# Down and query products with the weights stationary and the tokens moving, in one transformer block on one core

## The chip, the core and the metric

The kernel runs on one NeuronCore of a Trainium2 chip, as one launch. The metric is the device time of one execution in microseconds (us), measured outside the profiler. Beside it there is one profiled execution, whose trace is read here: the span runs from the first to the last instruction of the program. Everything is float32 in and out. Large products are made in float32r, a reduced form of float32, with each operand split in two exact halves (a high part and what is left of it), so that one float32 product is three float32r products: high by high, high by low, low by high.

## The reference, cut to what matters

One transformer block over 256 tokens of width 2048: a mixer (attention with three branches beside a gated linear recurrence) and then a feed-forward layer that picks 128 of 16,384 experts for each token. Only the feed-forward layer is touched. Its core:

```python
def peer_ffn(h, wq, keys, down, up):
    hf = h.reshape(T, D)                                            # T = 256, D = 2048
    q = (hf @ wq).reshape(T, PEER_HEADS, 2, PEER_DQ // 2)           # 8 heads, 2 halves, 128
    s = jnp.einsum('thpd,hpkd->thpk', q, keys)                      # 128 keys a half
    v1, i1 = lax.top_k(s[:, :, 0], 16); v2, i2 = lax.top_k(s[:, :, 1], 16)
    cand = v1[..., :, None] + v2[..., None, :]                      # 256 candidates a head
    vals, pick = lax.top_k(cand, 16)                                # -> expert rows eidx, softmax g
    act = gelu(einsum('td,thkd->thk', x, down[eidx])) * g
    out = einsum('thk,thkd->td', act, up[eidx])
```

The kernel does not gather rows of `down` and `up`. It multiplies all tokens by all 16,384 rows of `down`, takes the gelu, multiplies by a matrix of gate weights (expert by token, zero where an expert was not picked) and multiplies the result by all of `up`.

## The kernel before

**The stream of weights.** All weight matrices come from HBM in tiles of 128 x 2048 floats (`raw`, four buffers) that SyncE's queue loads. `next_part` splits each half of such a tile (a part: 128 x 1024, two chunks of 128 rows of the contraction by 512 columns) into `wh` (ScalarE copies with rounding, L197) and `wl` (VectorE subtracts, L198), three buffers each. `get` hands one part to the matmuls; `fill(AHEAD)` keeps two more ready.

**The products.** `block` makes one block of 512 columns for all 256 tokens: eight parts, and for each part `mm_sub` goes over two chunks and two halves of the tokens and calls `mm3`, three matmuls. The first operand of `T.matmul` after the output is the stationary one. In `mm3` it is a slice of the tokens (`xH` or `xL`, 128 contraction rows by 128 tokens) and the 512 columns of weights move, so a result lies as [128 tokens, 512 columns] in a PSUM bank, one bank for each half of the tokens. The products of the query (`wq`, four blocks) and of `down` (`d`, 32 blocks of 512 experts) are made this way; `up` (`u`) too, with `ah` and `al`, the activations, as stationary tiles.

**Behind the products.** The search for the best keys needs scores [token, key], whose contraction runs over a head's 128 query columns, and `up` needs the activations as [expert, token]. So both results are turned: `ev_wq` copies the two banks to SBUF (L1076), turns each in four transposes on TensorE (`transpose4`, L600), copies them back (L1083) and then makes the scores (L1087). `ev_d` takes the gelu of both banks (L1199), turns them in two groups of four transposes (L1207), and copies each group to `xT` (L1210). For the first 14 blocks (`LAG`), `xT` is stored in HBM (`xd`) until the gate weights are there, and loaded again later; for the others it stays in SBUF. `act` multiplies `xT` by the gate weights (L1232) and splits it into `ah` and `al`.

**The order of the work.** The program is written out in one order; the work behind the products is cut into steps (the `yield`s of a generator), put in a list of jobs by priority (`add`), and `tick`, called after every part, emits the next steps at a rate that depends on the kind of job (`RATES`). Priority 0 is `ev_wq`, `ev_d`, `ev_u`; 1 is the search on VectorE and `act`; 2 is `picks`; 3 is `w_build`, the gate weights (one-hot tables on VectorE and ScalarE, 256 float32 matmuls at L1184). The main loop makes four query blocks, 14 `down` blocks, and then in turn one `down` block and two half blocks of `up`, until `down` is done.

Of the kernel before, what the change touches and what calls it, by code (L numbers as in the profile page):

```python
# [7 lines left out]
F32 = mybir.dt.float32  # L8
# [57 lines left out]
def kernel(  # L66
# [110 lines left out]
    def load(most=RAWB):  # L177
        """Loads the stream ahead, as far as the rings allow."""
# [21 lines left out]
    def ada_load():  # L200
        """Loads ahead, as far as the rings allow."""
# [14 lines left out]
    def ada(m):  # L216
        """One chunk of a modulation vector: rows of the turned weights times the conditioning."""
        t = avs.pop(0)[1]
        V.scalar_tensor_tensor(out=t, in0=t, scalar=1.0, in1=cb, op0=OP.mult, op1=OP.mult, accum_out=m)  # L219
        n = pos["adl"]  # L220
        while (pos["adl"] < 2 * NDC or n - len(avs) > 2 * NDC) and ada_load():
            pass

    def ada_close(seg, k, n):
        """The biases; where it scales, one plus it, times the norm's gain."""
# [8 lines left out]
    def bg(r):  # L234
        """A share r of a chunk of the modulation vectors that VectorE makes beside the rest."""
# [14 lines left out]
    def adp_item():  # L250
        """A chunk of the rows of one modulation vector, in four column groups of the array."""
# [21 lines left out]
    def next_part():  # L273
        """Emits the next part of the stream; False at its end."""
# [56 lines left out]
    # steps per part of the stream, by the kind of work; the gate build's first steps go as fast as they may  # L331
# [8 lines left out]
    def finish(prio):  # L340
        """Runs the jobs up to that priority to their end."""
        while jobs and jobs[0][0] <= prio:
            step()
# [6 lines left out]
    def mm_sub(pst, kcs, wh, wl, first, last, aH, aL):  # L350
        for kk, kc in enumerate(kcs):
            for tb in range(NT):
                mm3(pst[tb], aH[:, kc, tbs[tb]], aL[:, kc, tbs[tb]], wh[:, kk], wl[:, kk],
                    first and kk == 0, last and kk == len(kcs) - 1)

# [13 lines left out]
    def rsqrt(pool, ss, n, w, name, parts=P, bufs=2):  # L369
        """1/sqrt(ss/n + eps) of a few columns, by Newton's method from an integer first guess."""  # L370
# [89 lines left out]
    def ada_first(n):  # L460
        """Chunks of the first two modulation vectors; the tokens' next two chunks when they are complete."""
# [12 lines left out]
    # two sets of four blocks, in turn over pieces of the width; the sums of the set that rests wait in SBUF  # L474
# [37 lines left out]
    def rest(b, name):  # L512
        """The rest of one of the first four blocks, added up in SBUF."""
# [18 lines left out]
    def mix(*gens, rate=0.0):  # L532
        """Steps of several pieces of work in turn."""
# [30 lines left out]
    # the compressed branch borrows what the later branches fill  # L564
# [4 lines left out]
    def table(i):  # L569
        """The rotation's tables with a norm's gains folded in."""  # L570
# [9 lines left out]
    def rope(dst, src, nh, cos, sin, name):  # L580
        """dst = src*cos + swap(src)*sin over nh heads of 128."""
# [129 lines left out]
    lw = rn.tile([P, 2, RB, P], F32, name="lw")  # L711
    G.dma_start(lw, lru_w)
    def recurrence(gr):
        n = RG
        if True:
# [19 lines left out]
            # d = 1/(1 + tanh) refined from (1 + exp)/2; decay 2d - 1; input sqrt(tanh) d (1 + ti) u  # L735
# [19 lines left out]
    held = {}  # L755

    def scores(sp, g, tb):
        """Unnormed weights of the causal and the windowed branch, and their sums."""
# [29 lines left out]
    def outputs(sp, g, tb):  # L788
        """The compressed branch's weights; all gated weights turned and times the values."""
# [281 lines left out]
    def ev_wq(j, pst):  # L1071
        """Scores of two heads; leaves them to the search."""
        res = []
        for tb in range(NT):
            qs = kq.tile([P, 512], F32, tag="qs", bufs=3, name=f"qs{j}{tb}")
            A.copy(qs, pst[tb])  # L1076
            res.append(qs)
        yield
        for tb in range(NT):
            tp = transpose4(res[tb], f"wq{j}{tb}")  # L1080
            yield
            qt = kq.tile([P, 512], F32, tag="qs", bufs=3, name=f"qt{j}{tb}")
            A.copy(qt, tp)  # L1083
            yield
            sx = ps_t(f"s{j}{tb}")
            for k in range(4):
                T.matmul(sx[:, k * P:(k + 1) * P], qt[:, k * P:(k + 1) * P], kt[:, 4 * j + k], start=True, stop=True)  # L1087
# [5 lines left out]
    def search(j, tb, sc):  # L1093
# [3 lines left out]
        # both lists are sorted: rank (a, b) has (a + 1)(b + 1) - 1 before it, so only those under 16 can be picked  # L1097
# [15 lines left out]
    def picks(tb):  # L1113
        """From places in the candidate lists to expert rows, and the softmax; heads and picks on partitions."""
# [5 lines left out]
        # place p of rank (a, b): a = max(p / 8 - 1, p / 4 - 6, 0), b = p - min(16 a, 8 a + 8, 4 a + 24)  # L1120
# [40 lines left out]
    def w_build():  # L1161
        """Gate weights by expert and token: per token the product of two one-hot tables."""
# [30 lines left out]
    xTt, wts, actH, actL = {}, {}, {}, {}  # L1193

    def ev_d(eb, pst):
        r = []
        for tb in range(NT):
            t = bp.tile([P, 512], F32, tag="ge", bufs=4, name=f"ge{eb}{tb}")
            A.activation(t, pst[tb], AF.Gelu)  # L1199
            r.append(t)  # L1200
        yield
        t = bp.tile([P, 4, S], F32, tag="xT", bufs=3, name=f"xT{eb}")
        for cc in range(2):
            tp = ps_t(f"xt{eb}{cc}")
# [207 lines left out]
```

## Time and profile before

| | |
|---|---|
| device time, median of 3 runs | 2092.45 us (2089.61 to 2093.78) |
| span of the profiled execution | 2090.6 us |
| what lies around the span, taken as median less span | 1.85 us |
| TensorE matmuls busy | 2025.0 us, 97% of the span |
| VectorE busy | 1449.4 us, 69% |
| ScalarE busy | 1053.0 us, 50% |
| moved to and from HBM | 507 MB, mean 243 GB/s |

The page of the profile gives the profiled execution by its span alone. Busy time of TensorE's matmuls is the time in which at least one matmul is in flight; a matmul's record is longer than the distance to the next one's start, so the cost of one in a row of them is read from start to start, not from its duration. PEld is the loading of stationary tiles, which has records of its own. L346 is line 346 of the kernel; a line of a helper such as `mm3` stands for all its callers, and the tile's name tells them apart.

### The profile page before, as it was taken

The page shows a single profiled execution, that of the slowest core. Times are in us where ns is not written, and L with a number is a line of the kernel's source. Part 1 is how long each engine was busy: PE and PEld are TensorE (multiplying, and loading weights), DVE is VectorE, ACT ScalarE, POOL GpSimd, SP SyncE. Part 2 cuts the span into 40 slices and gives each one's busy share as a digit, 9 for nine tenths or more (in the row PEclk, how much of TensorE's full clock was granted, in tenths as well). Part 3 has the DMA queues.
Part 4 walks back from the last instruction along what each step waited for, and adds up shares of the span by engine and source line. Part 5 has one row for each costly group of instructions (what it writes and reads, how often), then busy time and mean ns, then how long its engine had stood idle before and what let it go on. Part 6 is the DMA issues. An engine that isn't in the chain of part 4 may idle for free.

```text
span 2090.6 us, 24862 instructions
## 1 busy us (share of the span) xinstructions
PE 2025.0 (97%) x9434; PEld 1635.6 (78%) x9434; DVE 1449.4 (69%) x2149; ACT 1053.0 (50%) x1526; POOL 60.9 (3%) x95
## 2 busy tenths in 40 slices
PE   5999997999999999999999999999999999999998
PEld 4777664877888888887888888888888888888887
DVE  7888999887998666646667766665555555555566
ACT  3544676545456777854444444444444444444443
POOL 0000000000000000001000000000000000000000
PEclk8999998999999999999999999999999999999999
DMA  9897788994556666579777877765555565555563
GB/s 374 333 358 310 264 341 312 347 347 165 174 177 201 226 218 241 203 258 332 253 243 258 294 251 253 247 244 191 191 193 200 200 202 194 200 201 191 194 209 141
DMA packets 75849, 508.73 MB, mean 243 GB/s; under 512 B 8528, under 2 KB 9040, under 8 KB 20176
## 3 DMA queue, kind: packets, MB, share of 16 engines
q1 hardware_dynamic: 63792, 450.50, 60.5%
q0 software_dynamic: 11936, 56.63, 7.6%
q8 instruction: 74, 1.21, 0.2%
q14 instruction: 47, 0.39, 0.1%
HBM read 478.78 MB, written 28.31 MB: 243 GB/s over the span
## 4 chain that ended last, share of the span: by engine, by line
PE 86%; DVE 6%; issue 3%; DMA 3%; ACT 1%; POOL 0%; SPq 0%; DVEq 0%; POOLq 0%; ACTq 0%
PE d L348 11%; PE d L346 11%; PE d L347 11%; PE u L347 10%; PE u L348 10%; PE u L346 10%; PE w L1184 3%; DVE av L219 2%; DVE wl L198 2%; PE wq L346 1%; PE wq L347 1%; PE wq L348 1%; PE a L347 1%; PE a L348 1%; PE a L346 1%
## 5 line engine op out<-in xcount | busy, mean ns | idle before, releaser
L198 DVE TENSOR_TENSOR wl<-raw,wh 128x1024 fp32r<-128x1024 f32 x649 | 789.6, 1222 | 511.8 <-ACT wh L197 511.6
L197 ACT CAST wh<-raw 128x1024 fp32r<-128x1024 f32 x649 | 680.0, 1050 | 777.8 <-PE u L348 334.5
L346 PE MATMUL d<-wh,xH 128*128 128x512 f32 x1024 | 411.2, 402 | 0.0
L347 PE MATMUL d<-wl,xH 128*128 128x512 f32 x1024 | 405.1, 396 | 0.9 <-DVE wl L198 0.9
L348 PE MATMUL d<-wh,xL 128*128 128x512 f32 x1024 | 404.9, 395 | 0.0
L346 PE MATMUL u<-wh,ah 128*128 128x512 f32 x1024 | 402.1, 393 | 0.0
L347 PE MATMUL u<-wl,ah 128*128 128x512 f32 x1024 | 399.4, 390 | 1.3 <-DVE wl L198 1.2
L348 PE MATMUL u<-wh,al 128*128 128x512 f32 x1024 | 399.1, 390 | 0.0
L348 PEld LDWEIGHTS d<-wh,xL 128*128 128x128 f32 x1024 | 192.4, 188 | 45.8
L347 PEld LDWEIGHTS d<-wl,xH 128*128 128x128 f32 x1024 | 192.7, 188 | 43.9 <-DVE wl L198 1.3
L346 PEld LDWEIGHTS d<-wh,xH 128*128 128x128 f32 x1024 | 192.8, 188 | 42.6
L347 PEld LDWEIGHTS u<-wl,ah 128*128 128x128 f32 x1024 | 192.4, 188 | 41.8 <-DVE wl L198 3.0
L348 PEld LDWEIGHTS u<-wh,al 128*128 128x128 f32 x1024 | 192.2, 188 | 40.5
L346 PEld LDWEIGHTS u<-wh,ah 128*128 128x128 f32 x1024 | 192.3, 188 | 39.0
L219 DVE SCALAR_TENSOR_TENSOR av<-av,cb 128x2048 f32<-128x2048 f32 x64 | 146.0, 2285 | 5.4 <-DMA av<-in_ada_w_dram 5.4
L1168 DVE TENSOR_TENSOR oh<-con,idT 128x1024 f32<-128x1024 f32 x64 | 78.3, 1223 | 64.2 <-PE w L1184 64.2
L1189 ACT ACTIVATE oh<-oh,gT 128x128 f32<-128x128 f32 x256 | 83.7, 394 | 34.8 <-DVE oh L1168 34.5
L1256 DVE TENSOR_TENSOR acc<-acc,u 128x512 f32<-128x512 f32 x112 | 71.6, 681 | 0.0
L1184 PEld LDWEIGHTS w<-oh 128*128 128x128 f32 x512 | 65.5, 191 | 4.4
L1184 PE MATMUL w<-oh 128*128 128x128 f32 x512 | 66.6, 275 | 0.0
L346 PE MATMUL y<-wh,xH 128*128 128x512 f32 x128 | 52.1, 409 | 3.6 <-ACT xH L197 3.6
L346 PE MATMUL wq<-wh,xH 128*128 128x512 f32 x128 | 52.5, 410 | 2.5 <-ACT xH L197 2.5
(365 smaller groups left out, 2044.8 us busy)
## 6 DMA issues: line engine op xcount, KB each, us to landing
raw<-in_down_dram SPq DMA_DIRECT2D x128, 1024.0 KB, 5.0
raw<-in_up_dram SPq DMA_DIRECT2D x128, 1024.0 KB, 5.0
av<-in_ada_w_dram SPq DMA_DIRECT2D x64, 1024.0 KB, 7.1
raw<-in_w_a_dram SPq DMA_DIRECT2D x32, 1024.0 KB, 9.4
raw<-in_ada_p_dram SPq DMA_DIRECT2D x16, 1024.0 KB, 7.1
raw<-in_w_out_dram SPq DMA_DIRECT2D x16, 1024.0 KB, 7.9
raw<-in_wq_dram SPq DMA_DIRECT2D x16, 1024.0 KB, 5.0
wd<-stg POOLq DMA_DIRECT2D x8, 2048.0 KB, 8.0
```

The source lines that it names most:

```text
L197: A.copy(dst_h, src)
L198: V.tensor_tensor(dst_l, src, dst_h.bitcast(F32), OP.subtract)
L219: V.scalar_tensor_tensor(out=t, in0=t, scalar=1.0, in1=cb, op0=OP.mult, op1=OP.mult, accum_out=m)
L346: T.matmul(o, ah, bh, start=first, stop=False)
L347: T.matmul(o, ah, bl, start=False, stop=False)
L348: T.matmul(o, al, bh, start=False, stop=last)
L1168: V.tensor_tensor(oh, iota.unsqueeze(1).unsqueeze(1).to_broadcast([P, 4, 2, P]), idT[:, 4 * q:4 * q + 4].unsqueeze(3).to_broadcast([P, 4, ...
L1184: T.matmul(wps[p_][:, k * P:(k + 1) * P], oh[:, k, 1], oh[:, k, 0], start=True, stop=True)
L1189: A.activation(ohs[p_][:, k, 0], ohs[p_][:, k, 0], AF.Copy, scale=gT[:, t:t + 1])
L1256: V.tensor_tensor(a, a, pst[tb], OP.add)
```

## The change

Two functions are added. `mm_turn` makes the same products with the operands exchanged: a 128 x 128 slice of `wh` or `wl` is stationary, and the 256 tokens of a chunk of `xH` or `xL` move. The result of one block lies as [128 columns, 256 tokens] in each half of two PSUM banks. `turned` does what `block` does with it, for the four query blocks and the 32 `down` blocks. `ev_wq` and `ev_d` lose their transposes and one copy for each group: `ev_wq` copies the two banks and makes the scores from the copy, `ev_d` takes the gelu straight into `xT`. They have fewer steps. Nothing else is different (comments were taken out).

```diff
+    def mm_turn(pst, kcs, wh, wl, first, last, bH, bL):
+        for kk, kc in enumerate(kcs):
+            f, e = first and kk == 0, last and kk == len(kcs) - 1
+            for i in range(4):
+                o = pst[i // 2][:, i % 2 * S:i % 2 * S + S]
+                ws = slice(i * P, (i + 1) * P)
+                T.matmul(o, wh[:, kk, ws], bH[:, kc], start=f and i % 2 == 0, stop=False)
+                T.matmul(o, wh[:, kk, ws], bL[:, kc], start=False, stop=False)
+                T.matmul(o, wl[:, kk, ws], bH[:, kc], start=False, stop=e and i % 2 == 1)
+
+    def turned(name, ticks=1):
+        pst = [ps_x(f"{name}_{i}") for i in range(2)]
+        for sub in range(8):
+            wh, wl = get()
+            mm_turn(pst, (2 * sub, 2 * sub + 1), wh, wl, sub == 0, sub == 7, xH, xL)
+            fill(AHEAD)
+            tick(ticks)
+        return pst
...
     def ev_wq(j, pst):
-        res = []
-        for tb in range(NT):
-            qs = kq.tile([P, 512], F32, tag="qs", bufs=3, name=f"qs{j}{tb}")
-            A.copy(qs, pst[tb])
-            res.append(qs)
-        yield
-        for tb in range(NT):
-            tp = transpose4(res[tb], f"wq{j}{tb}")
-            yield
-            qt = kq.tile([P, 512], F32, tag="qs", bufs=3, name=f"qt{j}{tb}")
-            A.copy(qt, tp)
-            yield
+        qt = kq.tile([P, 4, S], F32, tag="qt", bufs=2, name=f"qt{j}")
+        for i in range(2):
+            A.copy(qt[:, 2 * i:2 * i + 2], pst[i].rearrange("p (k t) -> p k t", k=2))
+        yield
+        for tb in range(NT):
             sx = ps_t(f"s{j}{tb}")
             for k in range(4):
-                T.matmul(sx[:, k * P:(k + 1) * P], qt[:, k * P:(k + 1) * P], kt[:, 4 * j + k], start=True, stop=True)
+                T.matmul(sx[:, k * P:(k + 1) * P], qt[:, k, tbs[tb]], kt[:, 4 * j + k], start=True, stop=True)
...
     def ev_d(eb, pst):
-        r = []
-        for tb in range(NT):
-            t = bp.tile([P, 512], F32, tag="ge", bufs=4, name=f"ge{eb}{tb}")
-            A.activation(t, pst[tb], AF.Gelu)
-            r.append(t)
-        yield
         t = bp.tile([P, 4, S], F32, tag="xT", bufs=3, name=f"xT{eb}")
-        for cc in range(2):
-            tp = ps_t(f"xt{eb}{cc}")
-            for k in range(2):
-                for tb in range(NT):
-                    T.transpose(tp[:, k * S + tb * P:k * S + (tb + 1) * P],
-                                r[tb][:, (2 * cc + k) * P:(2 * cc + k + 1) * P], ident)
-            yield
-            A.copy(t[:, 2 * cc:2 * cc + 2], tp.rearrange("p (k t) -> p k t", k=2))
+        for i in range(2):
+            A.activation(t[:, 2 * i:2 * i + 2], pst[i].rearrange("p (k t) -> p k t", k=2), AF.Gelu)
+        yield
...
-        add(ev_wq(j, block(f"wq{j}", ticks=2)), 0)
+        add(ev_wq(j, turned(f"wq{j}", ticks=2)), 0)
...
-        add(ev_d(s, block(f"d{s}", ticks=2)), 0)
+        add(ev_d(s, turned(f"d{s}", ticks=2)), 0)
...
-                    add(ev_d(eb, block(f"d{eb}")), 0)
+                    add(ev_d(eb, turned(f"d{eb}")), 0)
```

## Rows read from the trace of the kernel before

**Rows 1.** The page: TensorE's, VectorE's and ScalarE's busy time in the whole span, and the span in 40 equal slices (52 us each) with the busy tenths of TensorE and the granted TensorE clock.

```profile
PE 2025.0 (97%) x9434; PEld 1635.6 (78%) x9434; DVE 1449.4 (69%) x2149; ACT 1053.0 (50%) x1526; POOL 60.9 (3%) x95
...
PE   5999997999999999999999999999999999999998
...
PEclk8999998999999999999999999999999999999999
```

**Rows 2.** The page: the chain of work that ended last, its shares of the span by engine.

```profile
PE 86%; DVE 6%; issue 3%; DMA 3%; ACT 1%; POOL 0%; SPq 0%; DVEq 0%; POOLq 0%; ACTq 0%
```

**Rows 3.** Waits of TensorE from 476 us (the first query matmul) to 2085 us (the last matmul): who waited for whom, us in total, times, longest.

```profile
PE wq L346 <- ACT xH L197: 2.5, 1, 2.5
PE u L347 <- DVE wl L198: 1.2, 2, 0.9
PE d L347 <- DVE wl L198: 0.9, 1, 0.9
```

**Rows 4.** Busy time of each engine in six stretches of the feed-forward layer: stretch, its length, busy time and count of each engine, granted clock, DMA share, GB/s.

```profile
480.00:560.00 80.00, 80.00 (x375) 65.53 (x374) 65.66 (x248) 40.25 (x51) 0.54 (x1) 1.00 0.52 180
560.00:660.00 100.00, 100.00 (x464) 81.12 (x463) 99.65 (x291) 52.19 (x66) 1.60 (x3) 1.00 0.56 187
660.00:920.00 260.00, 260.00 (x1422) 221.84 (x1421) 156.91 (x134) 198.46 (x423) 7.99 (x15) 1.00 0.60 215
920.00:1000.00 80.00, 78.69 (x353) 63.25 (x352) 50.05 (x65) 37.60 (x42) 15.04 (x22) 1.00 0.92 332
1000.00:1200.00 200.00, 199.15 (x879) 164.37 (x878) 143.02 (x159) 86.69 (x84) 10.18 (x14) 1.00 0.76 261
1200.00:2080.00 880.00, 879.92 (x3906) 718.84 (x3905) 510.65 (x529) 384.25 (x406) 17.39 (x22) 1.00 0.62 208
```

**Rows 5.** Groups of instructions by line and tile on TensorE, with their counts: matmuls of `down` and of the query (the first of the three lines of `mm3`; the other two have the same counts), the transposes of both, and the loads of the stationary tile of `down`.

```profile
L346 PE MATMUL d<-wh,xH 128*128 128x512 f32 x1024 | 411.2, 402 | 0.0
...
L346 PE MATMUL wq<-wh,xH 128*128 128x512 f32 x128 | 52.5, 410 | 2.5 <-ACT xH L197 2.5
...
L1207 PE MATMUL xt<-con,ge 128*128 128x128 f32 x256 | 38.5, 272 | 0.0
...
L600 PE MATMUL tp_wq<-con,qs 128*128 128x128 f32 x32 | 4.8, 272 | 0.0
...
L346 PEld LDWEIGHTS d<-wh,xH 128*128 128x128 f32 x1024 | 192.8, 188 | 42.6
```

**Rows 6.** TensorE's matmuls in order of time (start us, length us): the first and the last of the 96 matmuls of one `down` block, and the first and the last of 48 matmuls of half a block of `up`, both without anything between.

```profile
1226.57 0.39 PE L346 MATMUL d<-wh,xH 128*128 128x512 f32 x1
...
1248.73 0.40 PE L348 MATMUL d<-wh,xL 128*128 128x512 f32 x1
...
1260.81 0.39 PE L346 MATMUL u<-wh,ah 128*128 128x512 f32 x1
...
1271.47 0.40 PE L348 MATMUL u<-wh,al 128*128 128x512 f32 x1
```

**Rows 7.** The same view around one group of four transposes of a `down` block, which falls between matmuls of `up`.

```profile
1933.23 0.39 PE L348 MATMUL u<-wh,al 128*128 128x512 f32 x1
1933.47 0.60 PE L1207 MATMUL xt<-con,ge 128*128 128x128 f32 x4
1933.82 0.48 PE L346 MATMUL u<-wh,ah 128*128 128x512 f32 x1
1934.13 0.40 PE L347 MATMUL u<-wl,ah 128*128 128x512 f32 x1
```

**Rows 8.** The same view of the gate logits (`gl`, L890), whose matmuls have 24 columns of weights stationary and the 256 tokens of a chunk of `xH` or `xL` moving, in float32r: the first of 45 in a row, the two ends of an even stretch of ten among them, and the last.

```profile
264.38 0.28 PE L346 MATMUL gl<-xH,wh 128*24 128x256 f32 x1
...
265.99 0.28 PE L348 MATMUL gl<-xH,wl 128*24 128x256 f32 x1
...
267.01 0.28 PE L348 MATMUL gl<-xH,wl 128*24 128x256 f32 x1
...
269.42 0.28 PE L348 MATMUL gl<-xH,wl 128*24 128x256 f32 x1
```

**Rows 9.** Loads of full 128 x 128 stationary tiles close behind one another: eight float32 matmul records of the gate build with 128 moving columns each (order of time, merged), and 16 loads for float32 matmuls with 16 moving columns (the loads' own records, merged).

```profile
901.58 1.05 PE L1184 MATMUL w<-oh 128*128 128x128 f32 x8
...
273.96 1.86 PEld L795 LDWEIGHTS cs<-kcT,qT 128*128 128x128 f32 x16 [0.84 <-DVE kcT L693]
```

**Rows 10.** Groups of the same two kinds of matmul by their mean record, and of ScalarE's work behind the products.

```profile
L1184 PE MATMUL w<-oh 128*128 128x128 f32 x512 | 66.6, 275 | 0.0
...
L795 PEld LDWEIGHTS cs<-kcT,qT 128*128 128x128 f32 x32 | 3.7, 191 | 2.1 <-DVE pt L777 1.2 <-DVE kcT L693 0.8
...
L1199 ACT ACTIVATE ge<-d 128x512 f32<-128x512 f32 x64 | 37.9, 592 | 23.4 <-PE d L348 23.4
L1210 ACT COPY xT<-xt 128x512 f32<-128x512 f32 x64 | 37.0, 581 | 1.3 <-PE xt L1207 1.3
...
L1083 ACT COPY qt<-tp_wq 128x512 f32<-128x512 f32 x8 | 4.6, 578 | 0.0
```

More of the change, by code (lines that the diff above doesn't have):

```diff
@@ L1195, in ev_d @@
     def ev_d(eb, pst):
-        r = []
-        for tb in range(NT):
-            t = bp.tile([P, 512], F32, tag="ge", bufs=4, name=f"ge{eb}{tb}")
-            A.activation(t, pst[tb], AF.Gelu)
-            r.append(t)
-        yield
-        t = bp.tile([P, 4, S], F32, tag="xT", bufs=3, name=f"xT{eb}")
-        for cc in range(2):
-            tp = ps_t(f"xt{eb}{cc}")
-            for k in range(2):
-                for tb in range(NT):
-                    T.transpose(tp[:, k * S + tb * P:k * S + (tb + 1) * P],
-                                r[tb][:, (2 * cc + k) * P:(2 * cc + k + 1) * P], ident)
-            yield
-            A.copy(t[:, 2 * cc:2 * cc + 2], tp.rearrange("p (k t) -> p k t", k=2))
+        t = bp.tile([P, 4, S], F32, tag="xT", bufs=3, name=f"xT{eb}")
+        for i in range(2):
+            A.activation(t[:, 2 * i:2 * i + 2], pst[i].rearrange("p (k t) -> p k t", k=2), AF.Gelu)
+        yield
         if eb < LAG:
```

## The prediction, made before the changed kernel was run

> **What bounds the kernel now.** [...] A busy TensorE need not be the bound, so the chain of waits comes next: 86% of it is TensorE's own work [rows 2]. The waits of TensorE from the first query matmul to the last matmul say the same more sharply: 4.6 us in 1,608 [rows 3]. The reader is to see there that in the feed-forward layer no operand is late; each matmul starts when the one before lets it. So time is gained or lost here as the sum of TensorE's intervals, and ScalarE's and VectorE's part counts only where they would become late. Two stretches are near that [rows 4]: from 560 to 660 us VectorE is busy 99.65 of 100 us (the splits and the search for the best keys), and from 920 to 1000 us the DMA engines are at 0.92, where TensorE already loses 1.3 us.
>
> **The products.** The change touches 3 x 1024 matmuls of `down` and 3 x 128 of the query [rows 5]: 3,456 with 512 moving columns. Their price is the distance from start to start: 95 distances in 22.16 us, 233.3 ns each [rows 6]. In all 3,456 x 0.2333 = 806.3 us. They become 6,912 matmuls of 256 columns; as many columns move, and the stationary tiles are loaded twice as often. So the question is the distance s of a float32r matmul with 256 moving columns and a full 128 x 128 load before each. The trace has no such pair, but each half of it:
>
> - The moving half: the gate logits, 256 columns of the same `xH` and `xL` that will move, with a load of only 24 columns. 44 distances in 5.04 us: 114.5 ns. In their even stretch, nine in 1.02 us: 113.3 ns [rows 8]. That is half of the 226.8 ns of `up` (47 distances in 10.66 us) [rows 6], so halving the columns halves the price and there is no fixed cost for a matmul.
> - The loading half: 16 full loads for matmuls so short (16 columns) that only the loads can set the pace: 1.86 us less the last record's 0.191, over 15: 111.3 ns [rows 9, 10]. Eight matmuls of the gate build, each with a full load, give (1.05 - 0.275) / 7 = 110.7 ns [rows 9, 10]. A load's record lasts 188 ns [rows 5], but the next starts 111 ns after it.
>
> If load and stream run side by side, s is the larger of the two: 113.3 at the least, with 2 ns to spare for the load. They do run side by side for 512 columns: 188 ns of load under every 227 to 233 ns. The other end is in [rows 6] too: `down` and `up` move the same `wh` and `wl` under the same loads, and differ in the stationary tile alone, yet `down` takes 6.5 ns more for each matmul. If what costs this goes with each load from or beside `xH` and `xL`, it comes twice as often: s = 113.4 + 6.5, about 120. I take 114.5, the mean of the gate logits, as that is the row with the very operands that will move; 113.3 and 120 stay as ends. Sum at 114.5: 791.4 us, 14.9 less than now; at 113.3: 783.1, 23.2 less; at 120: 829.4, 23.1 more.
>
> [...]
>
> **The transposes.** 256 and 32 of them go [rows 5], in 72 groups of four. One group between matmuls of `up`: from the start of the last matmul before it to that of the second after it 0.90 us, where two plain distances are 0.454: 0.446 us for a group [rows 7, 6]. 72 x 0.446 = 32.1 us, all on TensorE and, with no waits there, all gained. They are replaced by nothing: the product already lies as the next step wants it.
>
> **What else goes or moves.** On ScalarE 64 copies of 581 ns and 8 of 578 go [rows 10], 41.8 us; the gelus and the copies of the query banks stay, with as many elements in as many instructions. ScalarE is half idle and TensorE doesn't wait for it in this layer after its first matmul [rows 3, 4], so this is nothing on the path. `ev_d` has two steps fewer, `ev_wq` four, so the jobs behind them (search, `picks`, gate build) are emitted some parts sooner; their work is the same. The DMAs are the same; the stores to `xd` on POOL's queue come two steps earlier in their block and pass nothing. VectorE's queue has the same instructions; a search step now stands a few places earlier among the splits, and TensorE waits for a split (`wl`) if it stands behind too many. Cover: two parts lie ready, some 5.5 us.
>
> **What eats into it.** From 560 to 660 us VectorE has 99.65 us of work in program order. TensorE's 100 us there hold some 33 parts of 12 x 0.2333 = 2.8 us beside transposes and scores; at 24 x 0.1145 = 2.75 us these parts are 91 us. So up to 9 us of gain would wait for VectorE, less the 5.5 that lie ready: I take 2.5. Between 920 and 1000 us the DMA engines are the limit and a faster TensorE only waits longer: the gain of these 80 us, at 47 us in 1,608 (3%), is 2.4, and I count 2.5 as lost. Together 5, bounds 0 and 12.
>
> **Sum**, against the profiled execution: 2090.6 - 14.9 - 32.1 + 5 = 2048.6, and with the 1.85 us by which the median lies above the span 2050.4. I predict 2050.
>
> **Rivals.**
> 1. *Each load costs the stream.* s = 120 as worked out: 829.4 - 806.3 - 32.1 = -9.0, with some 2 us eaten: 2085. For it: `down` is slower than `up` at equal shapes [rows 6], and some of the gate logits are as slow ((5.04 - 1.02) / 35 = 114.9 ns outside the even stretch). Against it: in the gate logits `xH` moves beside loads and nine in a row pay nothing [rows 8].
> 2. *The loads are not hidden*: this one is slower. Where a load can begin only some way into the matmul before, its 111 ns no longer fit into 113. The place is every one of the 6,912 matmuls; it decides from s = (806.3 + 32.1) / 6912 = 121.3 ns, 8 ns above what I take. At the full record of a load, 188 ns, the cost is 1299.5 - 838.4 = +461, so 2554; one after the other (111.3 + 113.3 = 224.6) it is +714, so 2806; a 130 that is just over the point gives +60, so 2152. For it: the slack is 2 ns, and no row has both halves at full size. Against: the gate build's 111 ns with a full load each [rows 9], though its stream is float32 of 128 columns. [...]
> 3. *Supply becomes the bound*: TensorE faster by 3 to 6% in `down` waits for splits or weights. A part costs VectorE 1.22 us and TensorE at least 2.7, and the DMA share is 0.62 in the long stretch from 1200 us on [rows 4]; so only the two stretches above can be hit. With double what I took, 10 us, it is 2055.
> 4. *The change doesn't do what it says* in time: the transposes hide in gaps. There are none [rows 3].
>
> **How the numbers follow.** s between 113 and 117, with supply as taken or somewhat worse (forecast and rival 3): 0.62. Rival 1, s from 117 to 121: 0.25. Rival 2: 0.12. Rival 4: 0.01. About 0.2% (4.2 us) is what a measurement of this kernel can tell from no change; s = 120.7 is the point. So faster: 0.62 and most of rival 1 (0.22), 0.84; the same: 0.04; slower: 0.12. Range: lowest is s = 113.3 with nothing eaten, 2090.6 - 55.3 + 1.85 = 2037; the upper end takes in rival 1, 2085 to 2088. Left out above: 0.14; below: 0.03.
>
> **What would show it.** In the profile after, `down` has 6,144 records of 128x256 whose starts lie 113 to 115 ns apart over a block; 120 is rival 1, over 121 rival 2. `xt` and `tp_wq` are gone. PEld's busy share goes up towards the whole span in `down`, as twice as many loads of 188 ns lie side by side; if its records get longer, the loads feel the stream. `up` keeps its 227 ns. Waits of TensorE for `wl` near 560 to 660 us show VectorE's share, and more loss than 1.3 us from 920 to 1000 us that of the DMA engines. What would make me wrong is s alone: 1 ns of it is 6.9 us, as much as all the rest is uncertain.

## The result, and the profile after

The changed kernel takes 2071.91 us (median of 4 runs, 2070.29 to 2073.24); the kernel before, run beside it on the same chip, takes 2093.11 (2089.61 to 2094.94). The ratio is 0.9902, with a 95% interval of 0.9888 to 0.9916: faster by 21 us, 1.0%. The prediction said faster, and 2071.9 lies inside its range, but the gain is half of the 42 us that the sum gave. The profiled execution has a span of 2068.5 us, against 2090.6.

The page of the kernel after: busy times, TensorE's share of 40 slices with the granted clock, and the shares of the chain that ended last (before: [rows 1, 2]).

```profile
PE 1998.7 (97%) x12602; PEld 1769.3 (86%) x12602; DVE 1451.6 (70%) x2149; ACT 1018.0 (49%) x1454; POOL 61.0 (3%) x95
...
PE   5999997998999999999999999999999999999998
...
PEclk8999998998999999999999999999999999999999
...
PE 75%; issue 10%; DVE 9%; DMA 4%; ACT 1%; POOL 1%; DVEq 0%; SPq 0%; POOLq 0%; ACTq 0%
```

TensorE is still busy for 97% of the span. It has 3,168 matmuls more (3,456 new ones less 288 transposes) and 26 us less of busy time. ScalarE's busy time is down by 35 us, which shows nowhere on the path. The chain gives TensorE less and issue more than before (86% and 3% there); most of that issue stands in long pieces between 985 and 1130 us, and TensorE is busy for 198.7 us of the 200 from 1000 us on (the stretches below), so it is no time that TensorE lost.

The costliest groups of the change, by line and tile. L363 to L365 are the three products of `mm_turn`; L1212 is the gelu that now writes `xT`.

```profile
L363 PE MATMUL d<-xH,wh 128*128 128x256 f32 x2048 | 577.7, 282 | 0.0
...
L363 PEld LDWEIGHTS d<-xH,wh 128*128 128x128 f32 x2048 | 385.1, 188 | 0.7
...
L1212 ACT ACTIVATE xT<-d 128x512 f32<-128x512 f32 x64 | 38.0, 594 | 29.9 <-PE d L365 29.9
```

The pace, the s of the prediction, is read from start to start. TensorE's matmuls of the kernel after in order of time (start us, length us): the ends of 115 and of 84 distances in the first 14 `down` blocks, the ends of the 191 distances of a later `down` block, and of 47 distances of `up` behind it (before: [rows 6]).

```profile
624.67 0.28 PE L363 MATMUL d<-xH,wh 128*128 128x256 f32 x1
...
638.21 0.28 PE L364 MATMUL d<-xL,wh 128*128 128x256 f32 x1
...
638.95 0.28 PE L363 MATMUL d<-xH,wh 128*128 128x256 f32 x1
...
648.75 0.27 PE L363 MATMUL d<-xH,wh 128*128 128x256 f32 x1
...
1309.71 0.28 PE L363 MATMUL d<-xH,wh 128*128 128x256 f32 x1
...
1331.99 0.28 PE L365 MATMUL d<-xH,wl 128*128 128x256 f32 x1
1332.11 0.39 PE L346 MATMUL u<-wh,ah 128*128 128x512 f32 x1
...
1342.79 0.39 PE L348 MATMUL u<-wh,al 128*128 128x512 f32 x1
```

13.54 us / 115 = 117.7 ns; 9.80 / 84 = 116.7; 22.28 / 191 = 116.6; `up` 10.68 / 47 = 227.2. So the new product takes 116.7 ns, half of the 233.3 that the old one took [rows 6], and in most of the first stage (the first 14 blocks, up to 955 us) a nanosecond more. No block shows the 113.3 of the gate logits [rows 8].

Waits of TensorE from 470 us to the end of the feed-forward layer: who waited for whom, us in total, times, longest (before: [rows 3]). The fourth line lies ahead of the first query matmul.

```profile
PE u L347 <- DVE wl L198: 3.3, 4, 1.6
PE pkT L1170 <- DVE sel L1162: 2.8, 3, 1.6
PE wq L363 <- ACT xH L197: 2.5, 1, 2.5
PE rbx L1052 <- DVE rsr_x L401: 2.1, 1, 2.1
PE d L365 <- DVE wl L198: 0.3, 1, 0.3
```

Busy time of each engine in the stretches of the feed-forward layer: stretch, length, PE, PEld, DVE, ACT, POOL, granted clock, DMA share, GB/s (before: [rows 4]).

```profile
560.00:660.00 100.00, 96.84 (x813) 95.50 (x813) 99.58 (x264) 50.93 (x72) 1.60 (x3) 1.00 0.54 185
660.00:920.00 260.00, 260.00 (x2226) 259.59 (x2225) 155.05 (x131) 188.22 (x391) 13.01 (x23) 1.00 0.66 237
920.00:1000.00 80.00, 78.40 (x489) 70.57 (x489) 52.82 (x68) 36.44 (x37) 10.64 (x15) 1.00 0.80 283
1000.00:1200.00 200.00, 198.69 (x873) 163.10 (x872) 143.35 (x161) 85.51 (x82) 9.62 (x13) 1.00 0.76 260
1200.00:2060.00 860.00, 859.48 (x5474) 780.48 (x5473) 507.21 (x525) 363.46 (x368) 17.39 (x22) 1.00 0.62 211
```

What was free of waits before now has some: 3.2 us are lost between 560 and 660 us, where VectorE is busy for 99.58 of 100 us, and TensorE's waits behind the first query matmul sum to 8.9 us (all lines but the fourth) against 4.6 [rows 3].

### The profile page after: what moved, and what is told of

Its sections match the earlier page's. It is cut to its first block, busy times and chain, and to the rows that moved or that the text cites. A ratio compares the mean times of both kernels' runs of the same rounds, so it can differ in the third digit from the quotient of the medians.

```text
span 2068.5 us, 31265 instructions
## 1 busy us (share of the span) xinstructions
PE 1998.7 (97%) x12602; PEld 1769.3 (86%) x12602; DVE 1451.6 (70%) x2149; ACT 1018.0 (49%) x1454; POOL 61.0 (3%) x95
## 4 chain that ended last, share of the span: by engine, by line
PE 75%; issue 10%; DVE 9%; DMA 4%; ACT 1%; POOL 1%; DVEq 0%; SPq 0%; POOLq 0%; ACTq 0%
PE d L363 10%; PE d L365 10%; PE d L364 10%; PE u L347 7%; PE u L348 7%; PE u L346 7%; PE w L1198 3%; DVE wl L198 3%; DVE av L219 2%; DMA raw<-in_ada_w_dram 2%; PE wq L363 2%; PE wq L364 2%; PE wq L365 1%; PE a L347 1%; PE a L348 1%
## 5 line engine op out<-in xcount | busy, mean ns | idle before, releaser
L363 PE MATMUL d<-xH,wh 128*128 128x256 f32 x2048 | 577.7, 282 | 0.0
L364 PE MATMUL d<-xL,wh 128*128 128x256 f32 x2048 | 573.0, 280 | 0.0
L365 PE MATMUL d<-xH,wl 128*128 128x256 f32 x2048 | 572.2, 279 | 0.3 <-DVE wl L198 0.3
L364 PEld LDWEIGHTS d<-xL,wh 128*128 128x128 f32 x2048 | 385.4, 188 | 0.7
L363 PEld LDWEIGHTS d<-xH,wh 128*128 128x128 f32 x2048 | 385.1, 188 | 0.7
L365 PEld LDWEIGHTS d<-xH,wl 128*128 128x128 f32 x2048 | 385.1, 188 | 0.5 <-DVE wl L198 0.5
L363 PE MATMUL wq<-xH,wh 128*128 128x256 f32 x256 | 73.2, 287 | 2.5 <-ACT xH L197 2.5
L364 PE MATMUL wq<-xL,wh 128*128 128x256 f32 x256 | 72.9, 285 | 0.0
L365 PE MATMUL wq<-xH,wl 128*128 128x256 f32 x256 | 72.5, 283 | 0.0
```

What stands on the lines that cost most here:

```text
L363: T.matmul(o, wh[:, kk, ws], bH[:, kc], start=f and i % 2 == 0, stop=False)
L364: T.matmul(o, wh[:, kk, ws], bL[:, kc], start=False, stop=False)
L365: T.matmul(o, wl[:, kk, ws], bH[:, kc], start=False, stop=e and i % 2 == 1)
```

## The experiments

The theory after the result: the transposes and the supply (what is lost to late weights and splits) went as forecast, and s is the one term that was off. Two questions follow: is that so, and what sets s? As rivals for the second, all three guesses of mine: (a) each load adds a fixed time, (b) the moving tokens go at that pace whatever the load, (c) the pace depends on where the tiles of the two operands lie in SBUF. The places of the tiles (bytes within a partition) are those that the kernel's allocation gives; no trace shows them: `xH` at 32576 and `xL` at 48960 (64 modulo 128), `wh` and `wl` from 98336 up and `ah`, `al` from 161824 up, in the kernel before from 170016 (all 32 modulo 128).

All runs in one table: median, ratio to the kernel before on the same chip with its 95% interval (none for a single run), and the distances read from the traces, from 1200 us on unless said otherwise; block 20 is apart there, and is told of with q24. A figure for the first stage is the mean of its `down` blocks, so a stretch shown below can differ from it by some tenths.

| run | time, us | ratio | `down`, ns | `up`, ns |
|---|---|---|---|---|
| before | 2093.11 | 1 | 233.3 | 226.8 |
| after | 2071.91 | 0.9902 (0.9888 to 0.9916) | 116.7 (first stage 117.7) | 226.9 |
| notrans | 2065.90 | 0.9875 (0.9852 to 0.9899) | 233.3 | 226.7 |
| a32 | 2078.50 | 0.9933 (0.9910 to 0.9955) | 117.8 | 227.1 |
| b32 | 2092.65 | 0.9995 (0.9983 to 1.0006) | 233.4 | 227.5 |
| a96 | 2088.87 | 0.9981 (0.9970 to 0.9993) | 120.0 (first stage 118.6) | 227.1 |
| a64 | 2092.51 | one run | 120.0 | 227.1 |
| a_up | 2113.36 | 1.0096 (1.0076 to 1.0115) | 120.0 | 233.4 |
| nt_up | 2093.11 | one run | 234.2 | 233.4 |
| half | 2080.01 | one run | 116.7 (first stage 118.5) | 226.9 |
| q24 | 2066.70 | one run | 116.7 (first stage 114.1) | 226.9 |
| b96 | 2090.48 | 0.9983 (0.9966 to 0.9999) | 232.4 | 227.3 |
| w64 | 2082.88 | one run | 118.3 | 227.2 |
| ordA | 2075.40 | 0.9912 (0.9895 to 0.9928) | 116.7 | 226.9 |
| ordB | 2072.78 | 0.9889 (0.9870 to 0.9909) | 116.7 | 226.9 |

**The transposes alone (notrans).** The changed kernel with the products made as before; the transposes stay left out.

```diff
-        add(ev_wq(j, turned(f"wq{j}", ticks=2)), 0)
+        add(ev_wq(j, block(f"wq{j}", ticks=2)), 0)
...
-        add(ev_d(s, turned(f"d{s}", ticks=2)), 0)
+        add(ev_d(s, block(f"d{s}", ticks=2)), 0)
...
-                    add(ev_d(eb, turned(f"d{eb}")), 0)
+                    add(ev_d(eb, block(f"d{eb}")), 0)
```

> The changed kernel's steps behind the products, but the products themselves as before (tokens stationary, 512 columns of weights moving): the transposes and their copies are left out and nothing takes their place, so the results lie turned the wrong way. It prices the two halves of the change one by one. If the prediction's terms hold but for s: removing the transposes alone gives 32 us less 5 for supply, 2066 us, and the exchange of operands then costs 6 us of the 2072. If supply (VectorE from 560 to 660 us, DMA from 920 to 1200 us) eats more than the 5 us: about 2072 us here too, and the exchange costs nothing.

The ends of one `down` block there, 95 distances apart:

```profile
1304.73 0.39 PE L346 MATMUL d<-wh,xH 128*128 128x512 f32 x1
...
1326.89 0.40 PE L348 MATMUL d<-wh,xL 128*128 128x512 f32 x1
```

22.16 / 95 = 233.3 ns, as before. The span is 2063.0 us: 2063.0 - 2090.6 = -27.6, where the prediction's terms for transposes and supply give -32.1 + 5 = -27.1. Its waits of TensorE from 470 us on:

```profile
PE u L347 <- DVE wl L198: 5.1, 2, 3.4
...
PE wq L346 <- ACT xH L197: 2.5, 1, 2.5
PE pkT L1170 <- DVE sel L1162: 1.5, 1, 1.5
```

They sum to 9.1 us against 4.6 [rows 3], so 4.5 of the 5 us for supply were lost, and some 32 us are left for the transposes: both terms hold. The exchange of the operands then takes 2068.5 - 2063.0 = +5.5 us by the spans (+6.0 by the medians), where the prediction had -14.9. By the times alone it is not settled that it costs anything, as the intervals of the two ratios overlap (from 0.9888 to 0.9899). The traces say more. The first query matmul, of the kernel after and of notrans:

```profile
474.56 0.80 PE L363 MATMUL wq<-xH,wh 128*128 128x256 f32 x2 [2.52 <-ACT xH L197]
```

```profile
477.02 0.79 PE L346 MATMUL wq<-wh,xH 128*128 128x512 f32 x1 [2.52 <-ACT xH L197]
```

The mixer, which is the same in both, was 2.5 us shorter in the profiled execution of the kernel after, so its feed-forward layer is longer by some 8 us. This separates the two parts of the change: the transposes carry all of the gain, and the exchange, far from giving 14.9 us, gives nothing and by the traces costs 5.5 to 8.

**The place of the tokens (a32, a96, a64; b32).** Small tables that were allocated behind `xH` and `xL` are allocated before them, in the changed kernel and (b32) in the one before, so that both lie 32, 96 or 64 bytes higher.

```diff
+    spl = cp.tile([P, RB], F32, name="spl")
+    hb = cp.tile([P, 2, RB], F32, name="hb")
     xH = cp.tile([P, NDC, S], F32R, name="xH")
```

(a32 and b32 have the first line alone, a64 the second alone, a96 both; the lines are taken away where they stood.)

> The changed kernel with one small table (32 bytes a partition) allocated ahead of the token tiles xH and xL, so that both start 32 bytes further on in every partition (at byte 96 of a 128-byte step where wh and wl start at byte 32; before they stood at 64). No instruction is different. Theory A (where the moving and the stationary tile lie to each other sets the pace of the stream, a cost for each moving column): the distance from matmul to matmul in down falls from 116.7 to about 113.3 ns, and the mixer's matmuls with xH stationary fall from 233 to 227 ns: 6912 x 3.4 = 23.5 us and some 1250 x 6.5 = 8 us, so about 2041 us. Theory B (the load of each stationary tile or the other engines' traffic costs the stream): nothing changes, 2072 us and 116.7 ns.

> The kernel before the change with the same 32 bytes ahead of xH and xL. Theory A: down falls from 233.3 to about 227 ns as up has it, and so do the query and the mixer: some 4700 matmuls x 6.5 ns = 31 us, about 2062 us. Then the 6.5 ns between down and up were already the place of the tiles, and never a cost of exchanging operands. Theory B: no change, 2093 us.

> The changed kernel with 96 bytes (two small tables) ahead of xH and xL: both then start at byte 32 of a 128-byte step as wh, wl, ah and al do. Theory A, if only the distance modulo 64 bytes counts: as with 32 bytes, 113.3 ns and about 2041 us. If the distance modulo 128 counts: one of the two is at 113.3 ns and the other stays at 116.7 (2072 us). Theory B: 2072 us.

> The changed kernel with 64 bytes ahead of xH and xL, the last of the four places in steps of 32 bytes (both start at byte 0 of a 128-byte step). The three others gave 116.7 (the change itself), 117.8 and 120 ns in down. If the cost goes with the low bits alone, one of the four places could be free of it: 113.3 ns and some 2047 us. If every place costs something as long as the tiles stand in these parts of SBUF: 116.7 to 120 again, 2070 to 2090 us.

In a96, the ends of 814 distances in the first stage (no other matmul between), and of the 191 of a later block:

```profile
863.42 0.28 PE L366 MATMUL d<-xL,wh 128*128 128x256 f32 x1
...
960.01 0.28 PE L367 MATMUL d<-xH,wl 128*128 128x256 f32 x1
...
1316.26 0.28 PE L365 MATMUL d<-xH,wh 128*128 128x256 f32 x1
...
1339.17 0.28 PE L367 MATMUL d<-xH,wl 128*128 128x256 f32 x1
```

96.59 / 814 = 118.7 ns, 22.91 / 191 = 119.9. Moving the tokens by 32 to 96 bytes changes the new product from 116.7 to 117.8 or 120.0 ns. The kernel is 17 us slower in a96; in a64, which ran once, 21 us, and the whole gain of the change is gone; the 7 us of a32 are not clear of the intervals. In the kernel before, 32 bytes change nothing that can be measured (233.4 ns in b32 against 233.3, ratio 0.9995). A fixed cost of each load, as in (a), does not do that. And a96 has two paces, 118.7 and 119.9 ns, with the same tiles at the same places: the place is not all that sets it.

Nor does the place of the tokens cost the gate logits anything. Those of a64 move the tokens from the same place as its `down` products do, past 24 columns of weights. After some twenty uneven distances they settle; the ends of an even stretch of ten:

```profile
269.53 0.28 PE L348 MATMUL gl<-xL,wh 128*24 128x256 f32 x1
...
270.66 0.28 PE L349 MATMUL gl<-xH,wl 128*24 128x256 f32 x1
```

1.13 us / 10 = 113 ns, as in the kernel before [rows 8]; the `down` products of a64, with 128 columns of weights, take 120.0.

**The weights beside the activations (a_up, nt_up).** The `wh` and `wl` of the feed-forward layer lie at the top of SBUF, from 204768 on, above `ah` and `al`, in the changed kernel and (nt_up) in notrans.

```diff
+        if high:
+            pool = high[0]
...
+    high.append(ctx.enter_context(tc.tile_pool(name="fp", bufs=1, side="right")))
```

> The changed kernel with the split weights wh and wl of the feed-forward layer in a pool of their own at the top of SBUF (from byte 204,768 of each partition; before at 98,336 to 122,912), where ah and al stand too (from 161,824). Nothing else is different. Moving xH and xL by 32 and 96 bytes has shown that the place of the tiles sets s: 116.7, 117.8 and 120 ns in down. Theory A' (a load taken from a stationary tile in the lower part of SBUF costs the stream, one from the upper part doesn't: up's 226.8 ns with ah, down's 233.3 with xH): s falls to 113.4 ns in down, some 6912 x 3.4 to 4 = 24 to 27 us, about 2047 us; up stays at 226.8. Theory C (only the low bits of the addresses count): the new place has the same low bits, so s stays at 116.7 and the time at 2072. Theory D (it is the moving operand's place): up, whose moving tiles are now up there, changes from 226.8.

> Products as before the change (tokens stationary, 512 columns of weights moving), no transposes (left out, so results lie the wrong way), and wh and wl at the top of SBUF. Against the run without transposes (2066 us, 233.3 ns in down): theory A' (the stationary tile's place counts; xH stays below): 233 ns and 2066 us. If what counts is that stationary and moving tile stand in different parts: down falls to about 227 ns, 21 us less, and up, whose two tiles are now both above, goes up to 233 ns.

One `down` block and one run of `up` of a_up, 191 and 95 distances:

```profile
1333.15 0.28 PE L366 MATMUL d<-xH,wh 128*128 128x256 f32 x1
...
1356.07 0.28 PE L368 MATMUL d<-xH,wl 128*128 128x256 f32 x1
...
1858.04 0.39 PE L349 MATMUL u<-wh,ah 128*128 128x512 f32 x1
...
1880.21 0.39 PE L351 MATMUL u<-wh,al 128*128 128x512 f32 x1
```

22.92 / 191 = 120.0 ns and 22.17 / 95 = 233.4 ns. `up`, which nothing else was done to, loses its faster pace when its moving tiles move, in both kernels (233.4 ns in a_up and in nt_up, 226.8 before). So the 6.5 ns between `down` and `up` on which rival 1 rested are no property of `xH`: they go with where the operands lie. The expectation of a_up has one thing wrong: the new place has the same low bits modulo 64 alone; modulo 128 it is 96 and no longer 32. So these two runs change the region and the low bits together and cannot tell one from the other.

**Shorter loads (half, q24).** In all but the first and last of a block's 16 chunks, 64 or 24 of the stationary tile's 128 columns are used.

```diff
+                if not (f or e):
+                    ws, o = slice(i * P, i * P + 64), o[0:64]
```

(q24: 24 in place of 64. The products of the other columns are left out, so neither computes the layer.)

> The changed kernel with stationary tiles of 64 columns instead of 128 in all but the first and last chunk of each block: half of the products of down and the query are left out, with as many matmuls, as many moving columns and loads half as long. Theory 1 (the load's length or its reads cost the stream 3.3 ns): s falls to between 113.3 and 115 ns as in the gate logits with 24 columns. Theory 2 (the moving tokens are read at 116.7 whatever the load does): s stays at 116.7 to 117.8 ns.

> The changed kernel with 24 of the 128 columns of the stationary tile in all but the first and last of each block's 16 chunks: the rest of these products (104 of 128 columns) is left out, the 256 moving tokens stay. The gate logits, from which the prediction took 114.5 ns, move the same xH and xL from the same places past stationary tiles of 24 columns, and settle at 113.3 ns. If the short loads are why, the down products fall from 116.7 to 113.3 ns here (6000 products x 3.4 to 4 ns, some 20 to 24 us, 2050 us); with 64 columns they had not fallen. If the length of the load plays no part, they stay at 116.7.

The loads of half and of q24, by groups:

```profile
L365 PEld LDWEIGHTS d<-xH,wh 128*64 128x64 f32 x1792 | 241.4, 135 | 0.0
```

```profile
L365 PEld LDWEIGHTS d<-xH,wh 128*24 128x24 f32 x1792 | 181.6, 101 | 24.2
```

In q24, the ends of 814 distances in the first stage (no other matmul between), and of the 191 of a later block:

```profile
858.00 0.28 PE L366 MATMUL d<-xL,wh 128*24 128x256 f32 x1
...
950.63 0.28 PE L367 MATMUL d<-xH,wl 128*128 128x256 f32 x1
...
1306.67 0.28 PE L365 MATMUL d<-xH,wh 128*128 128x256 f32 x1
...
1328.95 0.28 PE L367 MATMUL d<-xH,wl 128*128 128x256 f32 x1
```

92.63 / 814 = 113.8 ns, 22.28 / 191 = 116.6. Halving the load (135 ns of record in place of 188) leaves the pace where it was, in the first stage it is even 0.8 ns slower; only with 24 columns, whose loads take 101 ns, less than a product, is the pace of the gate logits there, and only in part of the kernel. So the load, or the narrower product that comes with it, does have a part, against (b), but not in proportion to its length, against (a). It also shows what was particular about the row that the prediction used: its stationary tiles had 24 columns.

Which part of the kernel that is, block 20 tells. It is one of the later blocks, but four float32 matmuls (`bc`) stand between its second and third product; block 21 starts behind `up`, as the other later blocks do. In q24 the last of what stands ahead of block 20's products, then the ends of 165 of its distances and of 167 of block 21, all with 24 columns:

```profile
1485.20 0.65 PE L410 MATMUL bc<-con,mod 128*128 128x128 f32 x4
...
1487.08 0.28 PE L367 MATMUL d<-xH,wl 128*24 128x256 f32 x1
...
1505.78 0.28 PE L367 MATMUL d<-xH,wl 128*24 128x256 f32 x1
...
1530.52 0.28 PE L365 MATMUL d<-xH,wh 128*24 128x256 f32 x1
...
1550.01 0.28 PE L367 MATMUL d<-xH,wl 128*24 128x256 f32 x1
```

18.70 / 165 = 113.3 ns and 19.49 / 167 = 116.7: the same tiles, loads of the same length, 25 us apart. In a96 the second half of block 20 goes at the 118.7 of the first stage, and its neighbours at 120.0; in the kernel after, both go at 116.7. So it is not the stage of the kernel, and a short load alone does not give 113.3. What the trace shows to differ between the two blocks is what stood ahead of the products; that this sets the pace is a guess, and no run was made to test it.

**Is it the place of the two to each other? (b96, w64)** b96 is the kernel before with the edit of a96. In w64 a 64-byte pad behind `xL` moves the weights and all that lies above, `ah` and `al` too, and leaves `xH` and `xL`.

```diff
     xL = cp.tile([P, NDC, S], F32R, name="xL")
+    pad = cp.tile([P, 16], F32, name="pad")
+    nc.vector.memset(pad, 0.0)
```

> The kernel before with xH and xL 96 bytes higher in their partition, so that they start at the same place within 128 bytes (32) as wh and wl do; nothing else differs. In all runs so far the products of up, whose stationary ah and al and moving wh and wl start at the same place within 128 bytes (32 and 32), go at 226.8 ns, and fall to 233.3 ns when the moving tiles start at 96 and the stationary ones at 32. If it is the place of the two operands to each other that sets the pace, the down and query products go from 233.3 to 226.8 ns: 3456 x 6.5 ns = 22 us, and the kernel takes some 2070 us. If it is the region of the memory that the tokens lie in, or their own place alone, the pace stays at 233.3 ns and the time at 2092.

> The changed kernel with all weight tiles (raw, wh, wl, and what lies above them, ah and al too) 64 bytes higher in their partition, xH and xL left where they were. If the place of moving to stationary tile within 128 bytes sets the pace, this is the case in which the tokens were moved 64 bytes up instead (the difference is the same, 32 bytes the other way), and the down products take 120.0 ns each, the time 2092 us. If the place of the tokens alone sets it, they stay at 116.7 to 117.8 ns, the time at 2072. The up products keep 226.8 ns by both, since both of their tiles move.

The ends of a `down` block, 95 distances of b96 and 191 of w64:

```profile
1313.41 0.40 PE L348 MATMUL d<-wh,xH 128*128 128x512 f32 x1
...
1335.49 0.40 PE L350 MATMUL d<-wh,xL 128*128 128x512 f32 x1
```

```profile
1316.95 0.28 PE L365 MATMUL d<-xH,wh 128*128 128x256 f32 x1
...
1339.55 0.28 PE L367 MATMUL d<-xH,wl 128*128 128x256 f32 x1
```

22.08 / 95 = 232.4 ns, not 226.8; 22.60 / 191 = 118.3 ns, neither 120.0 nor 116.7. Both forms of the idea fall: the difference of the two places within 128 bytes doesn't set the pace, and the tokens' own place alone doesn't either, since they did not move in w64. That a product whose moving tile stays goes from 116.7 to 118.3 ns when the stationary tile moves speaks for (c). Nor are these places within 128 bytes enough: a_up has the same as w64 (64 for the tokens, 96 for the weights) and goes at 120.0. At which places the pace would be the 113.3 of the gate logits, if at any, no run shows.

**The order of the products (ordA, ordB).** The same twelve products of a chunk in another order.

```diff
-                T.matmul(o, wh[:, kk, ws], bL[:, kc], start=False, stop=False)
-                T.matmul(o, wl[:, kk, ws], bH[:, kc], start=False, stop=e and i % 2 == 1)
+                T.matmul(o, wl[:, kk, ws], bH[:, kc], start=False, stop=False)
+                T.matmul(o, wh[:, kk, ws], bL[:, kc], start=False, stop=e and i % 2 == 1)
```

(This is ordB; ordA makes the four products of `wh` and `xH`, then the four of `wl` and `xH`, then the four of `wh` and `xL`.)

> The changed kernel with the order of the twelve products of a chunk changed: four with wh and xH, four with wl and xH, four with wh and xL, so that no stationary tile is loaded twice in a row and the same 256 tokens pass four times in a row. The same work, nothing left out. If load and moving tokens get into step with each other (the pace is a matter of which addresses are read beside each other), another order gives another pace, up or down, between 113.3 and 120 ns, and the time is 2051 to 2095. If the pace is a cost of the load alone, or of the moving tiles alone, it stays at 116.7 to 117.8 ns and the time at 2072.

> The changed kernel with the second and third product of each trio exchanged: wh and xH, wl and xH, wh and xL. The same work, nothing left out; two products in a row share the moving tokens in place of the stationary tile. If load and moving tokens get into step with each other, the pace differs from 116.7 to 117.8 ns (between 113.3 and 120, time 2051 to 2095); if not, it stays there, and the time at 2072.

In both, `down` stays at 116.7 ns from 1200 us on; in the first stage it goes at 116.8 in place of 117.7. So the order of the products within a chunk matters little: the step to another pace from 1200 us on, one of the two cases of the expectations, didn't come. What the first stage gained, 2,688 products by 0.9 ns or 2.4 us, doesn't arrive in the time (ratio 0.9889, within the interval of the change itself). The waits of TensorE in ordB from 470 us on show 1.1 us of it as longer waits of `up` (4.4 against 3.3), while the one for `sel` (the choice of the best keys) stays:

```profile
PE u L347 <- DVE wl L198: 4.4, 7, 1.8
PE pkT L1170 <- DVE sel L1162: 2.7, 3, 1.5
```

No run that computes the layer beats the changed kernel by more than the interval.

## Why the prediction was right, and where it failed

- **What bounds the kernel.** Right. TensorE's intervals add up to the time before and after; ScalarE lost 35 us of busy time (41.8 were forecast) and nothing came of it, as forecast.
- **The transposes: -32.1.** Right in kind and, with the supply, in size: -27.6 measured in notrans against -27.1. The `xt` and `tp_wq` groups are gone from the trace. No run parts the two terms; the waits in notrans do, with 4.5 us for supply and so some 32 for the transposes.
- **What eats into it: +5.** Right in size, not in detail. The waits went from 4.6 to 8.9 us. The 2.5 us for VectorE's full stretch were 3.2, and the wait is for the choice of the best keys (`sel`), one step of the search, not for the splits, which I had named. The 2.5 us for the DMA engines were less: TensorE idles 1.6 us there against 1.3 [rows 4], and 0.5 us more between 1000 and 1200 us.
- **The products: -14.9.** This is the step that failed: the choice of s = 114.5 ns. Measured is 116.7 in the 18 later blocks and 117.7 in the first 14; with as many products in each part (3,456, the query in the first), that is 117.2 on average, just outside the 113 to 117 that the prediction gave a chance of 0.62. 6912 x 117.2 = 810 us in place of 791: 19 of the 20 us between 42 and 22 in the spans. The working said that 1 ns of s is 6.9 us and that s alone could make it wrong; it took the value from the row "with the very operands that will move", and gave no price to what differed in that row, the stationary tile of 24 columns. q24 shows that this was part of it: with 24 columns, 113.3 to 113.8 ns is there in the same kernel; with 64 (half) or 128 it is in no block. It was not all of it, as 17 of the 18 later blocks go at 116.7 with 24 columns too.
- **The exchange had nothing to gain.** 2 x 116.7 = 233.3: two new products take what one old one took. Half of the row of `down` itself, with the same two regions of memory, and not that of the gate logits or of `up`, gives 116.7 at once, and with it a sum of 2090.6 - 32.1 + 5 + 1.85 = 2065, which notrans measures (2065.9). That it fits so well is luck of this placement: in the three others that ran in both forms, half of the old price is 1.1 to 3.8 ns below the new one (table at the end). The changed kernel lies 6 us above 2065.9. All distances that begin at a product of the query or of `down` sum to 825.3 us in the trace after and 817.0 in notrans; of these 8.3 us some 3.5 are the nanosecond of the first stage (3,456 x 0.95 = 3.3) and 1.7 a longer wait ahead of `pkT`, which is the wait for `sel`. The rest lies in the first products of the query, which run at a granted clock of 0.50 (for some 5.6 us there and 4.0 in notrans), and in the joins between kinds of matmul; it was not taken further apart.
- **Rival 1** (each load costs 6.5 ns, s = 120) is wrong in this kernel: at its placement twice the loads cost nothing from 1200 us on (2 x 116.7 = 233.3). But its pace is one that this product can have: 120.0 in a64, a_up and part of a96. That this placement is not one of them was luck, as no row before could tell.
- **Rival 2** did not come; s stayed below 121.3 in every placement tried. The load records stayed at 188 ns, and PEld is busy for 259.6 of 260 us from 660 to 920 us, as foretold. The sum of 2806, one after the other, is far from the 2071.91 measured. With loads of 101 ns the products go at 113.3 in some blocks and at 116.7 in others, with loads of 135 and 188 ns at 113.3 in none.
- **What stays open:** why 128 bytes of placement move the product between 116.7 and 120 ns, and why the same tiles go at 116.7 and 117.7 (after), 118.7 and 120.0 (a96) or 113.8 and 116.6 (q24) in two stretches of one kernel. It isn't the clock: the granted clock is 1.00 in both stretches of the three kernels. It isn't the stage either, as block 20 has the first stage's pace among the later blocks of a96 and q24. The runs show only that the pace differs with the places of the tiles, with the width of the stationary one and from one stretch to another; why, none shows, so the cause of s stays open.

## What to carry to other kernels

When a change multiplies a price by thousands, take the price from the row that agrees in all operands: moving width, stationary width and the memory that both come from; a row that agrees in the moving operand alone was 3 ns off here, and 3 ns were half the gain. If operands are exchanged and nothing else is known, start from half the distance of the product itself: here that was 116.7 ns, nearer to the 117.2 measured than the 114.5 of the gate logits, and the lower bound: in four placements the new product took 0 to 3.8 ns more. Build the two parts of a change apart (notrans): it shows at once which part carries the gain. And where a long stream runs at a strange pace, try other places for its tiles: here moves of the tokens by 64 and 96 bytes cost 17 to 21 us, though none that was tried gained any.

## What the runs showed of the hardware that was not expected

In these runs the pace of the full float32r products changes with where the tiles lie. For `xH` and `wh` at these places modulo 128 bytes, one product with 512 moving columns, and two with 256, take:

| `xH` / `wh` | one of 512, ns | two of 256, ns |
|---|---|---|
| 64 / 32 | 233.3 (before, notrans) | 233.3, first stage 235.3 (after) |
| 96 / 32 | 233.4 (b32) | 235.6 (a32) |
| 32 / 32 | 232.4 (b96) | 239.9, first stage 237.2 (a96) |
| 0 / 32 | not run | 240.0 (a64) |
| 64 / 96, `wh` at the top | 234.2 (nt_up) | 240.0 (a_up) |
| 64 / 96, all weights moved | not run | 236.6 (w64) |

In `down` the longer product hardly feels the place (232.4 to 234.2 ns), the shorter one does (116.7 to 120.0): two short products take from nothing to 7.5 ns more than one long one. Where the tiles of TensorE's own two operands lie is enough to change the short product by 3% (116.7 to 120.0), and `up` by 6.6 ns (226.8 to 233.4) when only its moving tiles lie elsewhere.

And one product, with the same tiles, has more than one steady pace: in q24 113.3 ns behind four float32 matmuls and 116.7 behind `up`, 25 us apart, at a granted clock of 1.00.
